# Rows turned in 32 by 32 squares: two of the kernel's transpose steps go from TensorE to transfers and VectorE

## The chip, the cores and the metric

The kernel runs on one core of a Trainium2 chip. The metric is the time of one execution on the device, in microseconds. The kernel before took 1190.43 us (median of three runs, 1189.83 to 1190.44). Its profile is that of one more execution, which took 1190.04 us.

The core has a matrix engine (TensorE, PE in the profile), a vector engine (VectorE, DVE), a scalar engine (ScalarE, ACT), a general one (GpSimd, POOL) and SyncE (SP), which here issues nearly all transfers. Each engine works through its own instructions in the order in which they were written; an instruction that waits holds up all that stand behind it on that engine. Transfers run on 16 DMA engines that all queues share.

## The reference

One layer of a hybrid decoder on 1024 tokens of width 1024, in float32:

```
h     = rmsnorm(x, mix_pre_norm)
proj  = h @ w_in                         # 1024 x 3584, split between two mixers
attn  = rmsnorm(dilated_mixture_attention(q_a, k_a, v_a), attn_out_norm)   # 512 wide
rec   = hgrn2_recurrence(q_h, f_h, i_h, g_h, ...)                          # 512 wide
mixed = concat([attn, rec]) @ w_out
x     = x + rmsnorm(mixed, mix_post_norm)
h     = rmsnorm(x, mlp_pre_norm)
ff    = square(relu(h @ w_ff1)) @ w_ff2   # inner width 4096
x     = x + rmsnorm(ff, mlp_post_norm)
```

Two places matter here. The product with `w_out` contracts over the 1024 columns of `[attn, rec]`, and the product with `w_ff1` over the 1024 columns of `h`. TensorE contracts over the partition axis, but both operands are made row by row, with tokens on partitions. So both have to be transposed first.

## The kernel before, in words

Every product is done in three passes: an operand is split into a high part (a rounded copy, by ScalarE) and a low part (the rest, by a VectorE subtraction). `split_into` (lines 85 to 87 before) does such a split; line 86 is the copy, line 87 the subtraction. `three_pass` (L90 to L92) is the three products.

Tokens are worked on in eight row blocks of 128, `t` = 0 to 7. The recurrence (`hgrn_core`, four heads) writes its gated rows to a buffer in device memory, `mix_dram` (L651), and the attention writes its own there too (`pair_rows`, L1134). The last quarter of the attention stays on the chip (`row_fin`).

The output stage is the loop over `t` from 0 to 7 after the attention (its steps are called step 0 to step 7 here). In step `t`, `late_out(t, 0)` and `late_out(t, 1)` multiply row block `t` with the two halves of `w_out`, 12 TensorE products each for the attention half, and 12 more each for the recurrent half where `t` is 4 or more. For `t` below 4 the recurrent half has been multiplied already during the attention (`early_out`, into `early_sum`). Between the two halves, `row_turn` makes the operands of the next row block: four TensorE transposes of 128 by 128 (L1208) into a PSUM bank, and a split of the bank.

Behind it, for each row, come a norm and the residual (`mixed_half`, `residual`, L1274 and L1275, on VectorE, with sums of squares on ScalarE and a power on POOL), the scaling for the feed-forward norm (`residual_b`, L1303, on VectorE), and `next_turn`: eight TensorE transposes (L1313) into two banks, and two ScalarE copies (L1319) into `hraw`, the transposed feed-forward operand. `split_tokens` splits it, 256 tokens at a time, into `h2`. Tables such as `RES`, `SCALE` and `TURN_END` say in which step each row has which of these done. Row 6 and row 7 are turned inside the first products of the feed-forward part (`mm1`).

After the loop, `mm1(0, 1)`, `mm1(1, 1)`, `mm1(0, 2)` and `mm1(1, 2)` are the first products with `w_ff1`, 12 instructions each, on tokens 0 to 511. The weight pairs that follow (`early_split(2)`, `early_split(3)`, written as wa2 and wa3) are split on ScalarE and VectorE; `early_mm(2, 1)` and `early_mm(3, 1)` use them. Tokens 512 to 1023 are split as `B22` after that.

A PSUM bank of `late_out` is used again by the row two steps later; for `t` of 4 or more it is free once `residual(t)` has read it. The order on all engines is the order in which the program is written out by hand; nothing moves instructions later. All loads and stores named here are issued by SP.

## Time and profile before

| | |
|---|---|
| median of three runs | 1190.43 us |
| profiled execution, its time | 1190.04 us |
| profiled execution, its span | 1188.1 us |
| TensorE busy | 1178.1 us (99%) |
| VectorE busy | 839.9 us (71%) |
| ScalarE busy | 548.9 us (46%) |
| POOL busy | 294.3 us (25%) |
| output stage and first feed-forward products | about 493 to 600 us of the span |

The span is the time from the first to the last instruction in the profile; the execution's own time has some 2 us beside it. In rows in order of time, the first number is the start in the span, the second a duration, both in us; `x8` is how many instructions were merged into the row, and what stands in brackets is idle time ahead of it and what ended it. Rows of groups give the duration as minimum, median and maximum in ns. Rows by stretch give, for PE, PEld, DVE, ACT and POOL in this order, the busy time and the number of instructions, and then the granted TensorE clock (1.00 is full speed), the share of the 16 DMA engines and GB/s.

### The profile page before, as it was taken

How to read it: one execution, taken by the hardware profiler on the slowest of the kernel's cores; microseconds unless marked ns; L12 is line 12 of the kernel's file. 1: busy time of each engine (PE TensorE's matmuls, PEld its weight loads, DVE VectorE, ACT ScalarE, POOL GpSimd, SP SyncE). 2: the span in 40 equal slices, each digit the busy share in tenths (PEclk: the TensorE clock that was granted, in tenths of full speed). 3: DMA queues.
4: the chain of work that ended last, by engine and by line, in shares of the span. 5: the costliest groups of instructions: out<-in, count | busy, mean ns of one | idle time of the engine just before them, and what ended most of it. 6: DMA issues, size and time to landing. Idle time of an engine off the chain costs nothing.

```text
span 1188.1 us, 17598 instructions
## 1 busy us (share of the span) xinstructions
PE 1178.1 (99%) x6486; PEld 1004.2 (85%) x6486; DVE 839.9 (71%) x1428; ACT 548.9 (46%) x1082; POOL 294.3 (25%) x282
## 2 busy tenths in 40 slices
PE   9999999999999999999999999999999999999997
PEld 9898989878888888888888888888888888888886
DVE  5686969686666667577697666675686653588796
ACT  7633424343666677764654222222244544434562
POOL 0112122001111010252503775667540000000022
PEclk9999999999999999999999999999999999999999
DMA  5222323147453644452425465554587524433337
GB/s 221 71 69 86 98 86 99 48 114 185 103 148 95 170 128 126 157 192 89 168 89 201 158 225 180 184 177 167 196 328 274 176 90 157 162 95 101 109 104 283
DMA packets 90549, 175.49 MB, mean 148 GB/s; under 512 B 14944, under 2 KB 42464, under 8 KB 90464
## 3 DMA queue, kind: packets, MB, share of 16 engines
q1 hardware_dynamic: 90320, 174.37, 45.4%
q8 instruction: 51, 0.84, 0.3%
q14 instruction: 34, 0.28, 0.1%
q10 hardware_dynamic: 144, 0.00, 0.0%
HBM read 116.91 MB, written 47.99 MB: 139 GB/s over the span
## 4 chain that ended last, share of the span: by engine, by line
PE 92%; ACT 3%; DVE 3%; issue 1%; DMA 0%; POOL 0%; DVEq 0%; POOLq 0%; ACTq 0%
PE f L2078 18%; PE f2s L2078 7%; PE pig L90 3%; PE pig L92 2%; PE pig L91 2%; PE pwo L90 2%; PE pwo L92 2%; PE pwo L91 2%; PE pl L536 1%; PE pm_ak L90 1%; PE pm_ak L92 1%; PE pm_ak L91 1%; PE pm_av L90 1%; PE pm_av L92 1%; PE pm_f L90 1%
## 5 line engine op out<-in xcount | busy, mean ns | idle before, releaser
L87 DVE TENSOR_TENSOR al<-ar,ah 128x1024 fp32r<-128x1024 f32 x56 | 70.7, 1262 | 79.7 <-ACT ah L86 77.4
L2078 PE MATMUL f<-bh,ah 128*128 128x512 f32 x320 | 124.5, 389 | 0.0
L2078 PE MATMUL f<-bl,ah 128*128 128x512 f32 x320 | 124.5, 389 | 0.0
L2078 PE MATMUL f<-bh,al 128*128 128x512 f32 x320 | 124.5, 389 | 0.0
L86 ACT ACTIVATE ah<-ar 128x1024 fp32r<-128x1024 f32 x56 | 59.1, 1056 | 86.8 <-DMA ar<-actd 86.4
L2078 PEld LDWEIGHTS f<-bh,ah 128*128 128x128 f32 x320 | 60.1, 188 | 12.6
L2078 PEld LDWEIGHTS f<-bl,ah 128*128 128x128 f32 x320 | 60.1, 188 | 12.5
L2078 PEld LDWEIGHTS f<-bh,al 128*128 128x128 f32 x320 | 60.1, 188 | 12.3
L2152 POOL TENSOR_SCALAR lbl<-ssq 128x1 f32<-128x1 f32 x4 | 3.3, 822 | 245.0 <-ACT fd L2148 244.8
L1701 POOL TENSOR_TENSOR e<-x,e 128x512 f32<-128x512 f32 x14 | 21.6, 1541 | 131.7 <-DVE x L1652 131.7
L2078 PE MATMUL f2s<-bh,al 128*128 128x512 f32 (+1 forms) x128 | 48.9, 382 | 0.0
L2078 PE MATMUL f2s<-bl,ah 128*128 128x512 f32 (+1 forms) x128 | 48.9, 382 | 0.0
L2078 PE MATMUL f2s<-bh,ah 128*128 128x512 f32 (+1 forms) x128 | 48.9, 382 | 0.0
L710 POOL TENSOR_SCALAR tout<-traw 128x256 f32<-128x256 f32 x16 | 19.2, 1199 | 103.0 <-DMA traw<-in_bias_tab_dram 100.2
L87 DVE TENSOR_TENSOR bl<-br,bh 128x1024 fp32r<-128x1024 f32 x32 | 40.1, 1255 | 1.1 <-ACT bh L86 1.0
L2095 ACT ACTIVATE acc<-f 128x512 f32<-128x512 f32 x28 | 16.7, 598 | 48.8 <-PE f L2078 48.8
L86 ACT ACTIVATE bh<-br 128x1024 fp32r<-128x1024 f32 x32 | 33.6, 1050 | 4.0 <-PE f L2078 3.0
L758 POOL TENSOR_TENSOR kl<-kf,kh 64x512 fp32r<-64x512 f32 x12 | 16.2, 1348 | 74.9 <-ACT kh L757 74.9
L90 PE MATMUL pwo<-woh,mt 128*128 128x512 f32 x80 | 32.2, 403 | 0.0
L87 DVE TENSOR_TENSOR wl<-raw,wh 128x1024 fp32r<-128x1024 f32 x21 | 25.7, 1224 | 8.6 <-ACT wh L86 8.6
L92 PE MATMUL pwo<-woh,mt 128*128 128x512 f32 x80 | 31.3, 391 | 0.0
L91 PE MATMUL pwo<-wol,mt 128*128 128x512 f32 x80 | 31.2, 390 | 0.0
(1725 smaller groups left out, 3882.7 us busy)
## 6 DMA issues: line engine op xcount, KB each, us to landing
ar<-actd SPq DMA_DIRECT2D x56, 512.0 KB, 3.6
br<-in_w_ff_dram SPq DMA_DIRECT2D x16, 1024.0 KB, 5.8
raw<-in_w_in_dram SPq DMA_DIRECT2D x28, 512.0 KB, 3.9
w1r<-in_w_ff_dram SPq DMA_DIRECT2D x14, 1024.0 KB, 6.4
actd<-e SPq DMA_DIRECT2D x17, 768.0 KB, 4.2
actd<-e SPq DMA_DIRECT2D x11, 1024.0 KB, 4.1
xr<-in_x_dram SPq DMA_DIRECT2D x8, 512.0 KB, 8.1
raw<-in_w_out_dram SPq DMA_DIRECT2D x8, 512.0 KB, 3.9
```

The lines of the kernel that those rows point to most:

```text
L86: S.activation(hi, src, AF.Copy)
L87: eng.tensor_tensor(out=lo, in0=src, in1=f32(hi), op=ALU.subtract)
L90: TE.matmul(dst, lhs[0], rhs[0], start=start, stop=False)
L91: TE.matmul(dst, lhs[0], rhs[1], start=False, stop=False)
L92: TE.matmul(dst, lhs[1], rhs[0], start=False, stop=stop)
L536: TE.matmul(pl[a:b, n, :96], kt[:, (4 * u + n) * P + a:(4 * u + n) * P + b], qs[:, :, 32 * g:32 * g + 32], start=True, stop=True, skip_gro ...
L710: G.tensor_scalar(by_class(dst[:, part_ * w:(part_ + 1) * w]), in_blocks(raw[:, FAR * DIL:]), 8.0, None, op0=ALU.mult)
L758: G.tensor_tensor(out=kl[a:b], in0=src, in1=f32(kh[a:b]), op=ALU.subtract)
L1701: eng[0].tensor_tensor(out=e1[:, 3], in0=a21, in1=e1[:, 2], op=ALU.add)
L2078: TE.matmul(pm, a[:, j, c], b[:, j, d], start=start and j == 0 and q == 0, stop=stop and j == 1 and q == 2, skip_group_check=True)
L2095: S.activation(acc_at(p, i), pm, AF.Copy)
L2152: G.tensor_scalar(base[:, t:t + 1], sums[j][:, t:t + 1], 1.0 / D, EPS, op0=ALU.mult, op1=ALU.add)
```

## The change

A transpose of 128 by 128 can be done in two steps: move its sixteen squares of 32 by 32 to their transposed places, and turn each square in itself. The change does the first step with transfers and the second with an instruction of VectorE that turns every 32 by 32 square of a tile (`V.transpose`, listed as STREAM_TRANSPOSE).

For the recurrent half of the mixer rows, the recurrence now writes to a buffer of its own (`rec_dram`), and `squares_load` reads it back in squares, in four transfers, one for each group of 32 partitions; a contiguous run is 32 floats, 128 B. This takes the place of a plain load. `row_turn` for that half becomes one turn on VectorE and a split that reads from SBUF. There is one `squares_load` for each two of rows 0 to 3 and one each for rows 4 to 7.

For the feed-forward rows 0 to 6, `residual_b` is followed by a store of the scaled row to device memory (`x2n_dram`). `lay_out` reads it back in squares, again in four transfers of 128 B runs, into the place where it was, and `square_turn` turns it on VectorE, in two instructions, right into `hraw`. Row 7 is still transposed by `next_turn`. `square_turn` stands later than `next_turn` did: rows 0, 1, 2 and 4 in the middle of the next step, row 3 at the end of step 6, row 5 after `mm1(0, 1)`, row 6 after `mm1(0, 2)`. The first `split_tokens` goes from step 5 to step 6.

```diff
@@ -254,8 +254,10 @@
 
     pick4 = cp.tile([P, DIL], F32, name="pick4")
     pick32 = cp.tile([P, 32], F32, name="pick32")
-    mix_dram = dp.tile([T, D], F32, name="mixd")
+    mix_dram = dp.tile([T, AW], F32, name="mixd")
+    rec_dram = dp.tile([T, AW], F32, name="recd")
     x2_dram = [dp.tile([P, D], F32, name=f"x2d{t}") for t in range(NT)]
+    x2n_dram = [dp.tile([P, D], F32, name=f"x2nd{t}") for t in range(NT - 1)]
 
     def ig_evac(hd, pm, blocks):
         for u, t in enumerate(blocks):
@@ -648,7 +650,7 @@
                 V.scalar_tensor_tensor(gate[:, n], pos[n // 4][:, n % 4], rs[:, n:n + 1], gate[:, n],
                                        op0=ALU.mult, op1=ALU.mult)
             if g2 == 3:
-                nc.sync.dma_start(out=mix_dram[:, h * P:(h + 1) * P].rearrange("(n p) d -> p n d", p=P), in_=gate)
+                nc.sync.dma_start(out=rec_dram[:, h * P:(h + 1) * P].rearrange("(n p) d -> p n d", p=P), in_=gate)
         if h == HH - 1:
             look(0, "N", 0)
             return gated
@@ -1129,7 +1131,7 @@
                         in1=recips[pr][:, :, b].rearrange("p h j -> p j h").unsqueeze(3).to_broadcast([P, 4, 2, 64]),
                         op=ALU.mult)
         if hf == 1:
-            to = mix_dram[:, AW + pr * P:AW + (pr + 1) * P].rearrange("(n i r) d -> r i n d", r=DIL, i=32)
+            to = mix_dram[:, pr * P:(pr + 1) * P].rearrange("(n i r) d -> r i n d", r=DIL, i=32)
             for r in range(DIL):
                 nc.sync.dma_start(out=to[r], in_=anats[pr][32 * r:32 * r + 32].rearrange("p n i d -> p n (i d)"))
 
@@ -1147,14 +1149,19 @@
     def early_rows():
 
 
-        early["rows"] = wide.tile([P, NE, AW], F32, tag="A", name="erows")
+        early["rows"] = wide.tile([P, NE // 2, 4, 2 * P], F32, tag="A", name="erows")
         early["table"] = wide.tile([P, 2, T], F32, tag="A", name="etable")
         early["order"] = early["table"][:, 1, :P]
         G.tensor_copy(early["order"].rearrange("p (i r) -> p i r", r=DIL), ident.rearrange("p (r i) -> p i r", r=DIL))
         early["mt"] = [wide.tile([P, 2, 2, 4, P], F32R, tag="A", name=f"emt{q}") for q in range(NE // 2)]
         for q in range(NE // 2):
-            nc.sync.dma_start(out=early["rows"][:, 2 * q:2 * q + 2],
-                              in_=mix_dram[2 * q * P:2 * (q + 1) * P, :AW].rearrange("(n p) d -> p n d", p=P))
+            squares_load(early["rows"][:, q], 2 * q, 2)
+
+    def squares_load(dst, t0, n):
+
+        src = rec_dram[t0 * P:(t0 + n) * P].rearrange("(b r) (j g f) -> g r j b f", r=32, g=4, f=32)
+        for g in range(4):
+            nc.sync.dma_start(out=dst[32 * g:32 * g + 32].rearrange("p j (b f) -> p j b f", f=32), in_=src[g])
 
     def early_sums():
         early["sum"] = [wide.tile([P, 2, D], F32, tag="A", name=f"esum{q}") for q in range(NE // 2)]
@@ -1164,11 +1171,14 @@
 
     def row_load(t):
         row = rows[t] = slab("S", f"row{t}")
-        c = AW if t < NE else 0
-        nc.sync.dma_start(out=row[:, c:AW + AL], in_=mix_dram[t * P:(t + 1) * P, c:AW + AL])
+        if t >= NE:
+            squares_load(rec_row(t), t, 1)
+        nc.sync.dma_start(out=row[:, AW:AW + AL], in_=mix_dram[t * P:(t + 1) * P, :AL])
 
     def rec_row(t):
-        return early["rows"][:, t] if t < NE else rows[t][:, :AW]
+        if t < NE:
+            return early["rows"][:, t // 2, :, t % 2 * P:(t % 2 + 1) * P]
+        return rows[t][:, :AW].rearrange("p (j c) -> p j c", j=4)
 
     def row_fin(t):
         return anats[-1][:, t].rearrange("p i d -> p (i d)")
@@ -1201,10 +1211,14 @@
                 mts[t] = slab("V8", f"mt{t}", F32R, (P, 2, 2, 4, P))
             dst = mts[t][:, which]
         mts[t, which] = dst
-        src = rec_row(t) if which == 0 else rows[t][:, AW:]
+        if which == 0:
+            V.transpose(rec_row(t), rec_row(t))
+            split_into(dst[:, 0], dst[:, 1], rec_row(t))
+            return
+        src = rows[t][:, AW:]
         pt = bank("pv" if late else tag, f"pmt{t}_{which}")
         for j in range(4):
-            piece = row_fin(t) if which == 1 and j == 3 else src[:, j * P:(j + 1) * P]
+            piece = row_fin(t) if j == 3 else src[:, j * P:(j + 1) * P]
             TE.transpose(pt[:, j * P:(j + 1) * P], piece, ident)
         split_into(dst[:, 0], dst[:, 1], pt.rearrange("p (j c) -> p j c", j=4))
 
@@ -1302,6 +1316,30 @@
             xress[t] = slab("S", f"x2n{t}")
         V.scalar_tensor_tensor(xress[t], xr, scales.pop(("x2", t)), gains["gmlp"], op0=ALU.mult, op1=ALU.mult)
 
+    def raw_room(t):
+        th = t // 4
+        if t % 4 == 0:
+            for kh in range(2):
+                hraw[kh, th] = wide.tile([P, 4, 512], F32, tag="A", name=f"hraw{kh}{th}")
+                if th == 0:
+                    h2[kh] = tuple(wide.tile([P, 4, 512], F32R, tag="A", name=f"h2{q}{kh}") for q in "hl")
+
+    def lay_out(t):
+
+        src = x2n_dram[t].rearrange("(a r) (k g f) -> g r k a f", a=4, g=4, f=32)
+        for g in range(4):
+            nc.sync.dma_start(out=xress[t][32 * g:32 * g + 32].rearrange("p (k a f) -> p k a f", k=NK, a=4), in_=src[g])
+
+    def square_turn(t):
+
+        xr = xress.pop(t)
+        th, c = t // 4, (t % 4) * P
+        raw_room(t)
+        for kh in range(2):
+            V.transpose(hraw[kh, th][:, :, c:c + P], xr[:, kh * 512:kh * 512 + 512].rearrange("p (k c) -> p k c", k=4))
+        if t == 4:
+            x_again(7)
+
     def next_turn(t):
 
         xr = xress.pop(t)
@@ -1312,10 +1350,6 @@
                 k = kh * 4 + j
                 TE.transpose(pt[:, j * P:(j + 1) * P], xr[:, k * P:(k + 1) * P], ident)
             src = pt.rearrange("p (j c) -> p j c", j=4)
-            if t % 4 == 0:
-                hraw[kh, th] = wide.tile([P, 4, 512], F32, tag="A", name=f"hraw{kh}{th}")
-                if th == 0:
-                    h2[kh] = tuple(wide.tile([P, 4, 512], F32R, tag="A", name=f"h2{q}{kh}") for q in "hl")
             S.activation(hraw[kh, th][:, :, c:c + P], src, AF.Copy)
 
     def split_tokens(kh, c):
@@ -1451,11 +1485,14 @@
     SCALE = {3: (0,), 4: (1,), 5: (2,), 6: (4,), 7: (5,)}
     SCALE_MID = {7: (6,)}
     SCALE_END = {5: (3,)}
-    TURN_MID = {6: (3,)}
-    TURN_END = {3: (0,), 4: (1,), 5: (2,), 6: (4,), 7: (5,)}
+    LAY_MID = {6: (3,)}
+    LAY_END = {3: (0,), 4: (1,), 5: (2,), 6: (4,), 7: (5,)}
+    TURN_MID = {4: (0,), 5: (1,), 6: (2,), 7: (4,)}
+    TURN_END = {6: (3,)}
 
     def scaled(r):
         residual_b(r)
+        nc.sync.dma_start(out=x2n_dram[r], in_=xress[r])
         if r + 3 < NT and r != 4:
             x_again(r + 3)
 
@@ -1480,23 +1517,23 @@
             x_again(t + 1)
         if NE <= t + 2 < NT:
             row_attn(t + 2)
-        if t in (5, 7):
+        if t in (6, 7):
             for kh in range(2):
-                split_tokens(kh, (t - 5) * P)
+                split_tokens(kh, (t - 6) * 2 * P)
         for r in RES.get(t, ()):
             residual(r)
+        for r in LAY_MID.get(t, ()):
+            lay_out(r)
+        mixed_half(t, 0)
         for r in TURN_MID.get(t, ()):
-            next_turn(r)
-        mixed_half(t, 0)
+            square_turn(r)
         late_out(t, 1)
         for r in SCALE_MID.get(t, ()):
             scaled(r)
         if t == NT - 1:
             w_get(W10 + 1, 0)
-        for r in TURN_END.get(t, ()):
-            next_turn(r)
-            if r == 4:
-                x_again(7)
+        for r in LAY_END.get(t, ()):
+            lay_out(r)
         if t + 3 < NT:
             row_norm(t + 3)
         if t == 4:
@@ -1506,6 +1543,8 @@
             residual(r)
         for r in SCALE_END.get(t, ()):
             scaled(r)
+        for r in TURN_END.get(t, ()):
+            square_turn(r)
 
 
 
@@ -1790,7 +1829,9 @@
     mm1(0, 1, "a", True)
     out_p1(0)
     residual(NT - 1)
-    mm1(1, 1, "a", True, lambda: next_turn(NT - 2), 1)
+    lay_out(NT - 2)
+    square_turn(NT - 3)
+    mm1(1, 1, "a", True)
     out_p1(1)
     small.add("S")
     residual_b(NT - 1)
@@ -1800,6 +1841,7 @@
     early_load(4)
     mm1(0, 2, "a", False)
     out_p2(0)
+    square_turn(NT - 2)
     for tag in ("T", "BT"):
         small.add(tag)
     mm1(1, 2, "a", False, lambda: next_turn(NT - 1), 2)
```

TensorE loses 88 instructions and its order is otherwise as before. On SP, the stretch that follows the loads of the last rows is, before, from row 3's `x2d` store on:

```order
L1293 DMA x2d_137<-xres_6034 128x1024
L1248 DMA xres_6288<-in_x_dram 128x1024
L1293 DMA x2d_138<-xres_6152 128x1024
L1248 DMA xres_6378<-in_x_dram 128x1024
L1293 DMA x2d_139<-xres_6288 128x1024
L1248 DMA xres_6493<-in_x_dram 128x1024
L1293 DMA x2d_140<-xres_6378 128x1024
```

Now, from row 3's scaled store on (`x2nd_146` to `x2nd_149` are the scaled rows 3 to 6, `x2d_140` and `x2d_141` the residuals of rows 5 and 6; `x4` is the four transfers of a row's squares):

```order
L1495 DMA x2nd_146<-esum_5161 128x1024
L1262 DMA xres_6360<-in_x_dram 128x1024
L1495 DMA x2nd_147<-xres_6150 128x1024
L1307 DMA x2d_140<-xres_6283 128x1024
L1331 DMA esum_5161<-x2nd_146 32x32x32 x4
L1331 DMA xres_6150<-x2nd_147 32x32x32 x4
L1495 DMA x2nd_148<-x2n_6495 128x1024
L1307 DMA x2d_141<-xres_6360 128x1024
L1262 DMA xres_6527<-in_x_dram 128x1024
L1495 DMA x2nd_149<-x2n_6554 128x1024
L1331 DMA x2n_6495<-x2nd_148 32x32x32 x4
```

Row 3's square loads stand behind the store of row 5's residual, and row 5's behind the store of row 6's scaled row. On VectorE, from the end of row 5's residual in step 6 on, there stood before:

```order
L1275 TENSOR_TENSOR xres_6288<-ad_6427,xres_6288 128x512
L1303 SCALAR_TENSOR_TENSOR x2n_6528<-xres_6288,x2r_6433,gmlp 128x1024
L87 TENSOR_TENSOR h2l_6091<-hraw_6089,h2h_6090 128x4x256
L87 TENSOR_TENSOR h2l_6100<-hraw_6098,h2h_6099 128x4x256
L1274 SCALAR_TENSOR_TENSOR ad_6534<-pwo_0_6380,prp_6498,gpost 128x512
```

Now the turns of rows 2 and 3 stand between (both in `esum_5161`):

```order
L1289 TENSOR_TENSOR xres_6283<-ad_6410,xres_6283 128x512
L1339 STREAM_TRANSPOSE hraw_6196<-esum_5161 128x4x128
L1339 STREAM_TRANSPOSE hraw_6199<-esum_5161 128x4x128
L1339 STREAM_TRANSPOSE hraw_6196<-esum_5161 128x4x128
L1339 STREAM_TRANSPOSE hraw_6199<-esum_5161 128x4x128
L1317 SCALAR_TENSOR_TENSOR x2n_6495<-xres_6283,x2r_6416,gmlp 128x1024
L87 TENSOR_TENSOR h2l_6198<-hraw_6196,h2h_6197 128x4x256
L87 TENSOR_TENSOR h2l_6201<-hraw_6199,h2h_6200 128x4x256
L1288 SCALAR_TENSOR_TENSOR ad_6502<-pwo_0_6362,prp_6463,gpost 128x512
```

Row 5's scaling, the splits and row 6's residual now stand behind row 3's turn. After the loop, from the end of row 7's residual on, VectorE had before:

```order
L1275 TENSOR_TENSOR xres_6493<-ad_6650,xres_6493 128x512
L1303 SCALAR_TENSOR_TENSOR x2n_6688<-xres_6493,x2r_6656,gmlp 128x1024
L87 TENSOR_TENSOR wa2l<-wr_6618,wa2h 128x1024
L87 TENSOR_TENSOR wa3l<-wr_6620,wa3h 128x1024
L87 TENSOR_TENSOR B220l<-hraw_6491,B220h 128x1024
```

Now it has, with the turn of row 5 (`x2n_6495`) and that of row 6 (`x2n_6554`):

```order
L1289 TENSOR_TENSOR xres_6527<-ad_6617,xres_6527 128x512
L1339 STREAM_TRANSPOSE hraw_6523<-x2n_6495 128x4x128
L1339 STREAM_TRANSPOSE hraw_6524<-x2n_6495 128x4x128
L1317 SCALAR_TENSOR_TENSOR x2n_6649<-xres_6527,x2r_6623,gmlp 128x1024
L87 TENSOR_TENSOR wa2l<-wr_6585,wa2h 128x1024
L1339 STREAM_TRANSPOSE hraw_6523<-x2n_6554 128x4x128
L1339 STREAM_TRANSPOSE hraw_6524<-x2n_6554 128x4x128
L87 TENSOR_TENSOR wa3l<-wr_6587,wa3h 128x1024
L87 TENSOR_TENSOR B220l<-hraw_6524,B220h 128x1024
```

Row 7's scaling (`x2n_6649`) stands behind row 5's turn, and the split of the weight pair wa3 behind row 6's.

## The prediction

> **What bounds the kernel now.** I read the page's busy times and chain first, then the busy times by stretch around the changed stage, then TensorE's and VectorE's rows in order of time, and last the transfers.
>
> ```profile
> span 1188.1 us, 17598 instructions
> PE 1178.1 (99%) x6486; PEld 1004.2 (85%) x6486; DVE 839.9 (71%) x1428; ACT 548.9 (46%) x1082; POOL 294.3 (25%) x282
> PE 92%; ACT 3%; DVE 3%; issue 1%; DMA 0%; POOL 0%; DVEq 0%; POOLq 0%; ACTq 0%
> 450.00:470.00 20.00, 19.44 (x135) 16.94 (x134) 14.82 (x43) 15.27 (x45) 0.80 (x2) 1.00 0.65 174
> 500.00:510.00 10.00, 10.00 (x50) 8.27 (x49) 5.55 (x8) 4.59 (x17) 4.44 (x11) 1.00 0.93 353
> 540.00:550.00 10.00, 10.00 (x50) 8.34 (x49) 8.02 (x10) 4.59 (x12) 2.34 (x5) 1.00 0.32 107
> 570.00:580.00 10.00, 10.00 (x51) 8.33 (x50) 5.47 (x7) 6.55 (x15) 4.11 (x8) 1.00 0.82 308
> ```
>
> TensorE is the bound: 92% of the chain, and from 500 us on it has no idle time in a stretch. So each microsecond taken out of its queue there is a microsecond of the kernel, and so is each microsecond for which it is made to wait: nothing behind the stage has slack in which a wait could vanish. VectorE is busy 55 to 80% of these stretches, and the DMA engines (the column before the last, as a share of 16) have room except around 500 to 510 us.
>
> **What is removed.** One step of eight transposes, and all transposes that go:
>
> ```profile
> 518.10 0.40 PE L92 MATMUL pwo<-woh,mt 128*128 128x512 f32 x1
> 518.33 1.04 PE L1313 MATMUL ph<-ident,esum 128*128 128x128 f32 x8
> 519.12 0.47 PE L90 MATMUL pwo<-woh,mt 128*128 128x512 f32 x1
> 519.44 0.39 PE L91 MATMUL pwo<-wol,mt 128*128 128x512 f32 x1
> L1313 PE MATMUL ph<-ident,esum x32: 272/272/273, 518.3 to 551.7; 128*128 128x128 f32 x32
> L1208 PE MATMUL pmt<-ident,erows x16: 272/273/329, 441.6 to 466.4; 128*128 128x128 f32 x16
> ```
>
> The listed 272 ns overlap, so cadence counts. A product follows the one before by 0.227 us (518.10 to 518.33); from 518.33 to 519.44 lie eight transposes and one product, 1.11 us, so eight transposes cost 0.885 us and four 0.44. Seven of eight feed-forward rows go (7 x 0.885 = 6.2) and the recurrent halves of rows 4 to 7 (4 x 0.44 = 1.76): **7.95 us** in the stage without idle time. The 16 for rows 0 to 3, another 1.8, lie at 441 to 466 us, where TensorE is 97% busy and VectorE gets 4 turns more (2.4 us by the price below). I bound this by -1.8 and +2.4 and take -0.5, nearer to TensorE's own row. The build shows 88 transposes fewer on TensorE, so that the change does not do what it says is no rival.
>
> **What a turn on VectorE costs.** The trace has no 32 by 32 turn. Nearest are operations from SBUF to SBUF:
>
> ```profile
> 510.68 0.41 DVE L1192 TENSOR_SCALAR row<-row,ara 128x384 f32<-128x384 f32 x1
> 515.64 1.28 DVE L1303 SCALAR_TENSOR_TENSOR esum<-xres,x2r,gmlp 128x1024 f32<-128x1024 f32 x1
> 553.34 0.69 DVE L1275 TENSOR_TENSOR xres<-ad,xres 128x512 f32<-128x512 f32 x1
> ```
>
> 384 elements a partition take 0.41 us and 512 take 0.69 (0.61 from start to start). I take 0.6 for 512, between 0.41 and 1.28. There are 8 for the mixer and 14 for the feed-forward rows, beside work on an engine with 20 to 45% free; where it is not free, it is in the walk below.
>
> **What a row in squares costs.** A feed-forward row is stored whole, and read back by four transfers of 1024 packets of 128 B: 4096 packets, 256 on each DMA engine. Rows for the price:
>
> ```profile
> x2d<-xres SPq DMA_DIRECT2D x8, 512.0 KB, 3.7
> traw<-in_bias_tab_dram SPq DMA_DIRECT2D x64, 32.0 KB, 2.1
> DMA packets 1139, 0.12 MB, mean 159 GB/s; under 512 B 1069, under 2 KB 1129, under 8 KB 1138
> DMA packets 1039, 0.52 MB, mean 268 GB/s; under 512 B 15, under 2 KB 1039, under 8 KB 1039
> ```
>
> The third row is the 0.75 us from 70.90 us, filled with packets of 4 B: 0.75 x 16 / 1139 = 10.5 ns each. The fourth is the 1.96 us from 120.90 us, 1024 packets of 512 B: 30 ns each. Between them by bytes, 128 B cost 15 ns, and 256 of them 3.9 us (2.7 to 7.7). A load of two packets an engine lands after 2.1 us, nearly all fixed. So the four land 2.0 + 3.9 = **5.9 us** after the first is issued (4.7 to 9.7), and none is issued before the store has landed, 3.7 us.
>
> The Trainium skill (DMA: Bandwidth & Descriptors, Specifications) says that below 512 B a transfer leaves line rate, by a read-modify-write. The trace has 17 GB/s an engine at 512 B, and 128 B at the price of 512 B would be my upper end, 9.7 us, and a sum near 1217.
>
> **Where the time goes: five waits of TensorE.** SP issues in order and VectorE works in order. A turn that waits for its row holds all VectorE work behind it, and a row's loads stand on SP behind stores that wait for VectorE. I walk through the order with the trace's durations: 0.13 for a hand-over, and for one half of an output row 12 products, 2.72 us (24 from row 4 on). The same walk without the change gives no wait.
>
> ```profile
> 550.73 1.09 ACT L86 ACTIVATE mt<-pmt 128x512 fp32r<-128x512 f32 x2 [2.14 <-PE pmt L1208]
> 552.57 0.74 DVE L1274 SCALAR_TENSOR_TENSOR ad<-pwo,prp,gpost 128x512 f32<-128x512 f32 x1
> 557.00 0.55 POOL L83 TENSOR_TENSOR x2r<-ms,nhalf 128x1 f32<-128x1 f32 x1
> 558.10 0.47 PE L90 MATMUL pwo<-woh,mt 128*128 128x512 f32 x1
> 560.59 2.36 DVE L87 TENSOR_TENSOR h2l<-hraw,h2h 128x1024 fp32r<-128x1024 f32 x2 [1.72 <-ACT h2h L86]
> 567.88 1.29 DVE L1303 SCALAR_TENSOR_TENSOR x2n<-xres,x2r,gmlp 128x1024 f32<-128x1024 f32 x1 [2.03 <-POOL x2r L83]
> 577.72 2.31 DVE L1303 SCALAR_TENSOR_TENSOR x2n<-xres,x2r,gmlp 128x1024 f32<-128x1024 f32 x1 [2.04 <-POOL x2r L83]
> 580.45 1.03 PE L1313 MATMUL ph<-ident,x2n 128*128 128x128 f32 x8
> 583.15 0.39 PE L1635 MATMUL f12a<-h2h,wa2l 128*128 128x512 f32 x1
> L86 ACT ACTIVATE h2h<-hraw x4: 1062/1066/1073, 539.0 to 560.4; 128x1024 fp32r<-128x1024 f32 x4
> ```
>
> One, step 4. Row 4's recurrent half is turned after the scaling that ends at 516.9, then copied by ScalarE (0.6) and subtracted (0.6): with hand-overs ready at 519.0. TensorE, without two batches of transposes, asks at 517.9: 1.1 us.
>
> Two, step 7. It begins at 558.10 now; 6.2 less of transposes and 1.1 of waiting make it 552.9. Its bank is freed by the first operation of row 5's residual (552.57 now), and the split of the first 256 tokens, 2.5 us, has moved from step 5 to right ahead of it. VectorE ends row 7's operands at 551.2 and the split at 553.7, the bank is free at 554.5: 1.6 us.
>
> Three, the first feed-forward product. Row 5's residual ends at 556.5, and only then can SP pass its store and issue row 3's loads: from 557.4 they land at 563.8 (5.9, and half a microsecond for row 4's beside them). VectorE holds row 3's turn since 557.7, nothing passes it, and turn, row 5's scaling (1.2) and the split end at 567.5. TensorE asks at 565.4: 2.1 us.
>
> Four, row 7's transposes (580.45 now). From 568.6 VectorE has row 6's residual (2.9), row 4's turn (1.2), 1.0 until POOL has row 6's scale, and its scaling, to 574.9. Row 6's store follows, and row 5's loads stand behind it on SP: issued at 575.7, landed at 582.2. Their turn is ahead of row 7's scaling, so row 7 is ready at 584.8. TensorE has done its three and a half products by 577.1: 7.7 us.
>
> Five, the second weight pair's product. Row 6's loads are issued after the store of row 7's residual, at 582.6, behind six weight loads of 512 KB. By the stretch 570 to 580 (308 GB/s at a share of 0.82) each takes 1.4 us of all engines, so the squares land at 595.0. Row 6's turn stands ahead of the pair's split on VectorE: ready at 597.5. TensorE comes there at 589.8: 7.8 us.
>
> Sum: 1.1 + 1.6 + 2.1 + 7.7 + 7.8 = 20.3 of waiting, less 7.95 and 0.5, is +11.9. The profiled execution took 1190.04 us, 0.39 below the median 1190.43 and inside the runs shown: 1190.0 + 11.9 = **1202 us**. Waits three to five each grow with the landing time one for one: at 4.7 us the sum is 1198, at 9.7 it is 1213, and 1217 with what then waits for banks as well. A turn of 0.4 instead of 0.6 takes 1.6 off; one of 1.28 adds some 5. The mixer's loads (2048 small packets each, around 500 us, where the share is already 0.93) delay the gains loaded behind them by 1 to 2 us; VectorE stands idle there for 3.0 us, which covers them:
>
> ```profile
> 504.14 0.69 DVE L87 TENSOR_TENSOR mt<-pmt,mt 128x512 fp32r<-128x512 f32 x1 [3.04 <-ACT mt L86]
> ```
>
> **Rivals.** *The loads are hidden*, 15%: no turn is ever waited for, and only 7.95 and 0.5 remain: 1181.6 us. For it: VectorE's free 20 to 45%, and half a step between most loads and turns. It holds only if rows 3, 5 and 6 land before VectorE reaches them; even at 4.7 us the walk has row 5's turn waiting 2 us and row 6's 8, which is why it has so little.
>
> *Half of it is covered*, 8%: if the last two turns stall VectorE but TensorE is made to wait only half as long as I say (10 instead of 20), loss and gain nearly cancel: 1190.0 + 10.2 - 8.45 = 1192 us.
>
> *The waits slow TensorE itself*, 15%: after each of the two long waits the next 12 products run at half speed, 5.4 instead of 2.7 us: 1202 + 5.4 = 1207 us. Against it: no row shows a slower clock, the clock column is 1.00 in all stretches; but no stretch has such a wait either. The Trainium skill (TensorE: Matmul & The Clock Gate, Part 1: The HAM clock gate) has this rule: after an idle window of about 3.4 us the clock halves, until some 3.4 us of work have passed. No run here shows it; by its own figure I estimate 1.7 us a wait, 1205 us.
>
> **Chances.** The five waits as walked 62%, halved clock 15%, hidden loads 15%, cancelled 8%. The five waits alone give 1197 to 1217; the range goes down to 1187 to take in the cancelled case, and leaves out the hidden one and a small part above. A difference under 0.2% (2.4 us) is not told from none by a measurement of this kernel; by the same cases faster has 17%, same 6%, slower 77%.
>
> **What would show it.** Right: TensorE idle between 550 and 610 us, with two gaps of several microseconds, at row 7's transposes and at the product with the second weight pair, ended by VectorE, and VectorE's own idle time there ended by the square loads. Landing of the four loads of a row near 6 us from the first issue; a 512-wide turn near 0.6 us; TensorE's busy time some 10 us smaller. Wrong: a gapless TensorE in that stretch (then the loads land early, or VectorE has more lead than I give it), turns above 1 us, or idle time around 425 to 510 us from the small packets, to which I gave nothing.

## The result, and the profile after

The changed kernel took 1206.66 us (median of four runs, 1206.17 to 1207.56), the kernel before 1190.41 beside it: a ratio of 1.0139 (95% interval 1.0126 to 1.0151), 1.4% slower. The forecast was 1202, with 1187 to 1217 as its range. The direction, the cause and the place of the wait that decides were as forecast. The 4.7 us that were missing are, to 0.1 us, TensorE's clock (2.9 us), which was a rival with 15%, and the end of that wait, 1.9 us later than the walk has it.

The profiled execution took 1206.17 us. Its page, with the engines' busy times and the chain of waits:

```profile
span 1204.4 us, 17517 instructions
...
PE 1176.6 (98%) x6398; PEld 998.2 (83%) x6398; DVE 848.5 (70%) x1450; ACT 542.3 (45%) x1068; POOL 289.1 (24%) x282
...
PE 49%; DVE 2%; SPq 1%; DMA 1%; issue 1%; ACT 0%; POOL 0%; DVEq 0%; POOLq 0%; ACTq 0%
```

TensorE has less work (88 instructions fewer), and the span is 16.3 us longer. The waits of TensorE between 540 and 610 us (who waits, for what; in sum, how often, the longest):

```profile
PE f13a L1674 <- DVE wa3l L87: 8.7, 1, 8.7
PE f11a L1672 <- ACT wh L86: 3.6, 1, 3.6
PE f11a L1674 <- DVE wl L87: 1.4, 1, 1.4
PE pwo L90 <- DVE ad L1288: 1.1, 1, 1.1
PE f10a L1673 <- DVE h2l L87: 0.5, 1, 0.5
```

And its busy time by stretch, with the granted clock in the third column from the right:

```profile
570.00:580.00 10.00, 5.03 (x14) 3.41 (x13) 8.21 (x11) 4.75 (x12) 2.91 (x6) 0.74 0.74 200
580.00:590.00 10.00, 10.00 (x47) 8.27 (x46) 3.70 (x4) 6.65 (x11) 2.90 (x5) 0.92 0.99 336
590.00:600.00 10.00, 1.34 (x5) 0.84 (x4) 3.76 (x4) 2.60 (x3) 8.09 (x7) 0.76 0.59 149
600.00:610.00 10.00, 10.00 (x34) 8.00 (x33) 5.97 (x6) 3.73 (x5) 0.00 (x0) 0.73 0.03 11
```

The gapless stage has two holes, at the second first-layer product (f11a, two waits one after the other) and at the third weight pair's (f13a, which waits for wa3l), and the clock column falls with each. The rows of TensorE in order of time show the price. Behind the second hole, products follow each other at 0.43 us instead of 0.23:

```profile
599.46 0.80 PE L1674 MATMUL f13a<-h2h,wa3l 128*128 128x512 f32 x1 [8.66 <-DVE wa3l L87]
600.05 0.63 PE L1672 MATMUL f13a<-h2h,wa3h 128*128 128x512 f32 x1
600.48 0.63 PE L1673 MATMUL f13a<-h2l,wa3h 128*128 128x512 f32 x1
...
605.55 0.39 PE L1673 MATMUL f12a<-h2l,wa2h 128*128 128x512 f32 x1
```

From 599.46 to 605.55 lie 14 products, 6.09 us; at 0.227 they take 3.18: 2.9 us lost. Behind the first hole's second wait 12 products from 576.27 to 581.56 take 5.29 instead of 2.72: 2.6 lost.

What sets the end of the long wait is not TensorE at all. The chain that ended last, in order of time (start, length, what; pieces of a few hundredths to 0.54 us between these are left out):

```profile
583.12 0.57 SPq L1331
...
583.74 4.77 SPq L1331
...
588.55 3.85 SPq L1331
...
592.45 3.67 DMA x2n<-x2nd
...
596.87 0.67 DVE hraw L1339
597.54 1.87 DVE wa3l L87
```

Row 6's four square loads (L1331) hold SP for 10 us behind the weight loads; the last lands at 596.1, VectorE turns the row, and only then splits the weights that TensorE has waited for since 590.8. VectorE's own rows show it, and the same for row 3:

```profile
564.12 1.30 DVE L1339 STREAM_TRANSPOSE hraw<-esum 128x512 f32<-128x512 f32 x2 [4.89 <-DMA esum<-x2nd]
...
596.24 1.30 DVE L1339 STREAM_TRANSPOSE hraw<-x2n 128x512 f32<-128x512 f32 x2 [10.28 <-DMA x2n<-x2nd]
```

### The profile page after: what moved, and what is told of

It is laid out like the page before. It is cut to its first block, busy times and chain, and to the rows that moved or that the text cites. A ratio compares the mean times of both kernels' runs of the same rounds, so it can differ in the third digit from the quotient of the medians.

```text
span 1204.4 us, 17517 instructions
## 1 busy us (share of the span) xinstructions
PE 1176.6 (98%) x6398; PEld 998.2 (83%) x6398; DVE 848.5 (70%) x1450; ACT 542.3 (45%) x1068; POOL 289.1 (24%) x282
## 4 chain that ended last, share of the span: by engine, by line
PE 49%; DVE 2%; SPq 1%; DMA 1%; issue 1%; ACT 0%; POOL 0%; DVEq 0%; POOLq 0%; ACTq 0%
PE f L2120 18%; PE f2s L2120 7%; SPq L1331 1%; DMA x2n<-x2nd 1%; DVE ad L1288 0%; DVE xres L1289 0%; DVE h2l L87 0%; DMA x2d<-xres 0%; DMA esum<-x2nd 0%; PE f13a L1674 0%; DVE x2n L1317 0%; DVE hraw L1339 0%; PE f13a L1673 0%; PE f13a L1672 0%; DVE wa3l L87 0%
## 5 line engine op out<-in xcount | busy, mean ns | idle before, releaser
L2120 PEld LDWEIGHTS f<-bh,ah 128*128 128x128 f32 x320 | 60.1, 188 | 12.4
L2120 PEld LDWEIGHTS f<-bl,ah 128*128 128x128 f32 x320 | 60.1, 188 | 12.4
```

The lines of the kernel that those rows point to most:

```text
L2120: TE.matmul(pm, a[:, j, c], b[:, j, d], start=start and j == 0 and q == 0, stop=stop and j == 1 and q == 2, skip_group_check=True)
```

## The experiments

Twelve kernels, each beside the kernel before on the same chip. The medians of before were 1190.39 (first four runs), 1190.20 (next four) and 1190.24 us (last four). None leaves a part of the computation out.

**1. Is the slow clock the idle time's work?** Extra products, thrown away, fill both holes:

```diff
+        for _ in range(fill):
+            TE.matmul(pm, ops1[q - 1][1][0][:, :P], part_of(b, 0)[0], start=True, stop=True, ...)
...
-    mm1(1, 1, "a", True)
+    mm1(1, 1, "a", True, fill=25)
...
-            mm1(q, 1, "a", True)
+            mm1(q, 1, "a", True, fill=48 if q == 3 else 0)
```

> The changed kernel, with extra products that are thrown away where TensorE stands still: 25 (5.7 us) ahead of the product that waits for the second weight pair's split at 570 us, and 48 (10.9 us) ahead of the one that waits from 590.6 to 599.5. Nothing else is changed and nothing is left out. Theory A, idle time slows TensorE's clock: the products behind both waits now follow each other at 0.227 us instead of 0.427, the clock column is 1.00 in all stretches, and the time falls by 2.9 us only, to 1203.8: the 2.6 us that the first wait's clock cost are eaten by the second wait, whose end VectorE sets. Theory B, the slow products have another cause (the transfers that run beside them): they stay slow, and the time stays at 1206.7.

Measured: 1205.73 us. The clock was full in all stretches, but only 0.9 us came back: the fill ended at 601.6, 1.3 us behind the split, and VectorE waited 1.7 us for a gain vector (until 510.5 us), for which it does not wait in the changed kernel's trace. So it was run again with 40 instead of 48.

> As the run with thrown-away products in the two gaps, but 40 instead of 48 in the second, so that they end at 599.8 us, just before the split that TensorE waits for there (600.3), and not 1.3 us behind it (601.6) as measured. Theory A, the clock behind the last wait costs 2.9 us: full clock everywhere, a wait of under 1 us at that product, and 1203.8 us (1203 to 1205). Theory B, the clock's loss is covered by something later: 1205.7 or more again, at a full clock.

Measured: 1204.45 us (1203.46 to 1205.62), 2.2 us under the changed kernel. The stretch of the first hole:

```profile
570.00:580.00 10.00, 10.00 (x46) 8.26 (x45) 8.33 (x11) 4.04 (x10) 2.90 (x6) 1.00 0.61 189
```

And TensorE's rows behind the second fill:

```profile
600.58 0.39 PE L1674 MATMUL f13a<-h2h,wa3h 128*128 128x512 f32 x1
600.81 0.39 PE L1675 MATMUL f13a<-h2l,wa3h 128*128 128x512 f32 x1
```

0.23 us a product, and the same transfers beside it: the idle time slows the clock, theory B falls. That 5.5 us of lost clock are worth 2.2 and not 5.5 is the second reading: what TensorE gains behind the first hole it loses in the second, whose end VectorE sets. That the last 2.9 did not come back whole has a reason in the same trace: the split was ready at 600.9, 1.5 us later than in the changed kernel.

**2. Is the 8.7 us wait a place in SP's queue?** Row 6's loads ahead of the four raw weights:

```diff
     early_load(3)
+    lay_out(NT - 2)
     for q in range(2):
         q_raw[q] = [small.get(f"w1r{q}{f}") for f in range(2)]
...
-    lay_out(NT - 2)
     square_turn(NT - 3)
```

> The changed kernel, with row 6's four square loads issued ahead of the four 512 KB loads of the raw first weights (and of row 7's residual store), right behind the two weight loads that are split next. Theory A, the 8.7 us wait is a place in SP's queue: the squares land near 587 instead of 596 us, the wait for the third weight pair's split falls below 1 us, no clock is lost behind it, and the time is 1195 (1193 to 1198). Theory B, small packets are what is slow, wherever they stand: they land at 593 or later, the wait shrinks by 3 us at most, and the time is 1203 or more.

Measured: 1200.10 us (ratio 1.0080, 1.0063 to 1.0097). SP's rows for row 6's loads and for the raw weights behind them:

```profile
580.44 5.16 SPq L1331 DMA_DIRECT2D x2n<-x2nd  x4
585.64 2.75 SPq L1829 DMA_DIRECT2D w1r<-in_w_ff_dram  x4
```

VectorE's row for its turn:

```profile
589.85 1.30 DVE L1339 STREAM_TRANSPOSE hraw<-x2n 128x512 f32<-128x512 f32 x2 [3.52 <-DMA x2n<-x2nd]
```

And TensorE's waits between 540 and 640 us, those under 1 us left out:

```profile
PE f11a L1672 <- ACT wh L86: 3.6, 1, 3.6
PE f13a L1674 <- DVE wa3l L87: 1.4, 1, 1.4
PE pwo L90 <- DVE ad L1288: 1.3, 1, 1.3
PE f10c L1672 <- ACT wf01h L86: 1.0, 1, 1.0
```

The wait fell from 8.7 to 1.4 and took its slow clock with it, so its cause is the place, as theory A says; the time lies between the two theories. For the row landed at 589.7, not 587, the raw weights that had to make room came some 4 us later (POOL begins their sums at 592.3 instead of 588.0), and these sums now hold TensorE up at f10c. A transfer that is moved ahead pushes another one back: 6.6 us were won, not the 11.7 expected.

**3. Which rows have no lead?** (A row has a lead when its squares land before VectorE reaches its turn.) Rows 3, 5 and 6 back on TensorE, at their places of before:

```diff
-    LAY_MID = {6: (3,)}
-    LAY_END = {3: (0,), 4: (1,), 5: (2,), 6: (4,), 7: (5,)}
+    LAY_MID = {}
+    LAY_END = {3: (0,), 4: (1,), 5: (2,), 6: (4,)}
...
-    TURN_END = {6: (3,)}
+    TURN_END = {}
...
+        if t == 6:
+            next_turn(3)
...
+        if t == 7:
+            next_turn(5)
...
+    mm1(1, 1, "a", True, lambda: next_turn(NT - 2), 1)
```

> The changed kernel, with rows 3, 5 and 6 turned on TensorE at their places of before; rows 0, 1, 2 and 4 and the recurrent half stay in squares. Theory A, only these three rows have no lead: the waits of 3.6, 1.4, 8.7 and 0.5 us and both stretches of slow clock are gone, one of 1.1 us may stay. Against before: +1.7 for rows 0 to 3 of the mixer (measured up to 466 us), -1.8 for rows 4 to 7, -3.5 for four rows, +1.4 of small waits, so 1188 us (1187 to 1190). Theory B, VectorE's added work as such holds TensorE: waits of several us between 550 and 590 remain, and the time is above 1192.

Measured: 1188.63 us (ratio 0.9984, 0.9975 to 0.9993). Two waits are left between 540 and 640 us, 0.6 and 0.2 us, at a full clock. These three rows are the whole loss, 18 us; the four with a lead pay.

**4. What do rows 0 to 3 of the mixer cost?** The same, with their recurrent half loaded plainly and transposed on TensorE.

> As the run before it (rows 3, 5 and 6 on TensorE), and the recurrent half of rows 0 to 3 on TensorE as well, with plain loads. What is left in squares: the recurrent half of rows 4 to 7 and feed-forward rows 0, 1, 2 and 4. Theory A, the turn of rows 0 to 3 costs VectorE more than it saves TensorE: 1.7 us less than the run before it, 1186.5 (1185 to 1188), TensorE's shift at 466 us is 0. Theory B, the 1.7 us came from the 4096 small packets on the DMA queues around 422 to 440 us or chance: still gone, since those are gone too; but if rows 0 to 3 gain what their 16 transposes take (1.8 us), it is 1.8 us slower, 1190.

Measured: 1186.94 us (ratio 0.9971, 0.9960 to 0.9982), 1.7 us less than run 3, as theory A says; TensorE's rows are shifted against those of before by 1.5 us more at 475 us than at 440 us in run 3, and by 0.1 here. To see why, the changed kernel's group of operations on that tile, how long ScalarE then waited for the turn (erows), and VectorE for ScalarE's copy (emt):

```profile
L1215 DVE STREAM_TRANSPOSE erows<-erows x4: 699/702/712, 442.9 to 468.4; 128x512 f32<-128x512 f32 x4
L86 ACT ACTIVATE emt<-erows x4: 629/630/634, 443.6 to 469.2; 128x512 fp32r<-128x512 f32 x4
...
  DVE erows L1215: 3.5, 4
  ACT emt L86: 2.8, 4
```

VectorE turns for 0.70 us and then stands still for 0.70 (2.8 in four) until ScalarE's copy is done, because the other half of that split is next in its order. So each turn and the wait behind it take 1.4 us. Not all of that is the change's: before, where TensorE transposes, VectorE already stands still at the same splits, by its waits from 440 to 475 us:

```profile
DVE emt L87 <- ACT emt L86: 2.2, 3, 0.9
```

The change adds 2.8 us of turns and 0.6 of standing still, on an engine that is busy 82% from 442 to 470 us (22.94 of 28.00 us; not the 97% of the expectation below). The test is to turn one step of the attention loop earlier, on the kernel of run 3:

```diff
-        45: lambda: wo_half(1, 1),
+        45: lambda: [wo_half(1, 1), rec_turn(0)],
...
-        49: lambda: [load_bias(AH - 1), wo_half(3, 0)],
+        49: lambda: [load_bias(AH - 1), wo_half(3, 0), rec_turn(1)],
+        51: lambda: rec_turn(2),
+        53: lambda: rec_turn(3),
```

> As the run with feed-forward rows 3, 5 and 6 on TensorE and all mixer rows in squares (1188.6 us measured), but VectorE turns the recurrent half of rows 0 to 3 one step of the attention loop ahead of the split that uses it. Theory A: in the changed kernel VectorE turns for 0.7 us and then stands still for 0.7 us, since next on it is the second half of the split, which waits for ScalarE's copy; with the turn ahead, the 0.7 us of standing still go, TensorE's shift at 466 us falls from 1.7 to 0.9 or less, and the time to 1187.8. Theory B, only the turn's own time on a VectorE that is 97% busy there counts, or the loads: 1188.6, as measured.

Measured: 1187.40 us, 1.2 us less. The same group there:

```profile
L1209 DVE STREAM_TRANSPOSE erows<-erows x4: 701/704/712, 442.1 to 466.1; 128x512 f32<-128x512 f32 x4
...
  ACT emt L86: 0.7, 2
```

The turn costs what it did; the standing still fell from 2.8 to 0.7 us, and TensorE's shift from 440 to 475 us from 1.5 to 0.1. The small packets are all still loaded in this run, so they were not the cause: most of the 1.7 us was the order, not the turn. But the 16 transposes taken off TensorE there, 1.8 us by the prediction's price, pay nothing even so.

**5. The recurrent half alone.** The kernel before with only `squares_load` and the turns of the eight mixer rows:

> The kernel before with the recurrent half of all eight mixer rows in squares and nothing of the feed-forward rows: all of these on TensorE as before. Theory A, this half of the change cancels in itself: +1.7 us for rows 0 to 3, -1.8 for rows 4 to 7, +0.3 for one wait: 1190.6 (1190 to 1191.5), no idle time of TensorE above 1 us after 490. Theory B, the 8192 small packets around 500 to 520 us delay the gains and rows too: waits there, and 1192 or more.

Measured: 1191.88 us (ratio 1.0014, 1.0005 to 1.0024), 1.3 above the forecast of theory A and just below that of theory B. Two waits of TensorE, 0.7 us at 546 (VectorE's residual is late) and 0.6 at 559 (ScalarE's copy of a transposed row is late), ate what rows 4 to 7 saved. VectorE does wait 1.0 us for a gain at 509 us, but it stands idle for 4.1 us more before that late residual, so theory B is near in time without its reason.

**6. Three tries to keep more rows in squares.** Row 5 late (run 4's kernel with row 5's turn behind the third pair's split); all squares with only the order mended; and rows 0 to 5 in squares with row 3's loads ahead of row 5's residual and row 5's turn late. The order in the second one:

```diff
+        for r in LAY_MID.get(t, ()):
+            lay_out(r)
         for r in RES.get(t, ()):
             residual(r)
-        for r in LAY_MID.get(t, ()):
-            lay_out(r)
...
     early_split(3)
+    square_turn(NT - 3)
+    square_turn(NT - 2)
     out_p2(1)
```

> As the run with rows 3, 5 and 6 and the mixer's rows 0 to 3 on TensorE (1186.9 us measured), but row 5 is in squares again, with its turn on VectorE moved behind the split of the third weight pair, where nothing of the first products waits for it. Theory A, a late row is harmless when no other work stands behind its turn: one batch of transposes less, 0.9 us, so 1186.1 (1185.5 to 1187). Theory B, its four loads, ahead of the weight loads on SP, delay these: a wait of 1 to 3 us for the second or third pair's split, and 1187.5 or more.

> The changed kernel with all its squares, three places changed: row 3's loads are issued ahead of row 5's residual instead of behind it, row 6's ahead of the four raw first weights (as in the run that gave 1200.1), and the turns of rows 5 and 6 stand behind the split of the third weight pair. Theory A, the loss lies in the order on SP and VectorE alone: the waits of 3.6, 1.4 and 8.7 us and the slow clock are gone; what stays is 1.7 us for rows 0 to 3 of the mixer and some 2 us where the raw weights come later; less 8.0 for all transposes: 1187 (1185 to 1190). Theory B, small packets and VectorE's added turns have no room in this stage: waits of more than 5 us in sum remain, and it is above 1192.

> Rows 0 to 5 of the feed-forward part in squares, row 3's loads ahead of row 5's residual, row 5's turn behind the split of the third weight pair; row 6, and the recurrent half of rows 0 to 3, on TensorE. Theory A: against the run with rows 3, 5 and 6 on TensorE (1186.9) two batches less, 1.8 us: 1185.2 (1184.5 to 1186.5), with no wait of TensorE above 1 us between 550 and 600. Theory B, row 3 is late even so: VectorE waits at its turn, the first product waits for the split behind it, and the time is 1187 or more.

Measured: 1188.68 us (ratio 0.9989, 0.9979 to 0.9998), 1197.27 (1.0055, 1.0040 to 1.0070) and 1189.64 (0.9995, 0.9985 to 1.0004). All three missed theory A, by 2.6, 10 and 4.4 us. The order alone gives back 9.4 us of the 16 (1206.66 to 1197.27), and then the waits sit elsewhere. The longest waits of TensorE in the second kernel:

```profile
PE f14a L1672 <- ACT wa4h L86: 1.7, 1, 1.7
PE f11a L1674 <- DVE wl L87: 1.4, 1, 1.4
PE f11a L1672 <- ACT wh L86: 1.2, 1, 1.2
PE f10c L1672 <- ACT wf01h L86: 1.0, 1, 1.0
```

And what ScalarE waited for there:

```profile
ACT wa4h L86 <- DMA wr<-in_w_ff_dram: 3.8, 1, 3.8
ACT wf01h L86 <- POOL s L1862: 3.8, 1, 3.8
```

Weight loads that stand behind the squares come late (wa4, and wf01 by way of POOL's sums): theory B's figure was the nearer one there. In the last kernel row 3 was still 1.6 us late for VectorE; but TensorE's longest wait in the first and the last is not at the squares' next user, as theory B had it. TensorE waits for the weight split of f11a: 1.2 and 1.4 us for its second half (wl), and in the last kernel 1.1 more for its first (wh). VectorE's and ScalarE's work of that step decides, and a transpose taken off TensorE there makes it wait longer: in run 4, with row 5 on TensorE, the same wait is 0.3 us, 0.9 less than in the first.

**7. The best of it.** Run 4's kernel with the turns of rows 4 to 7 ahead of the feed-forward scaling, so that ScalarE copies while VectorE scales; and, beside it, feed-forward rows 0, 1, 2 and 4 alone:

```diff
+        if NE <= t + 1 < NT:
+            rec_turn(t + 1)
         for r in SCALE.get(t, ()):
             scaled(r)
```

> As the run with rows 3, 5 and 6 and the mixer's rows 0 to 3 on TensorE (1186.9 us measured), but the recurrent half of rows 4 to 7 is turned ahead of the feed-forward scaling of that step instead of behind it, so that ScalarE's copy runs beside the scaling. Theory A, the 0.75 us for which VectorE waits for this copy in each step come back as earlier splits: the waits of 0.2 to 0.3 us at 520, 571 and 577 go, 1186.3 (1185.8 to 1187). Theory B, these waits have another cause: 1186.9.

> Feed-forward rows 0, 1, 2 and 4 in squares, everything else on TensorE: the recurrent half is loaded plainly and transposed on TensorE for all rows. Theory A, the recurrent half of rows 4 to 7 pays beside the feed-forward rows what TensorE's order shows, 0.44 us a row: 1188.4, 1.5 us slower than with it (1186.9). Theory B, it pays nothing, as the run with the recurrent half alone suggests (1191.9, of which rows 0 to 3 explain 1.7): 1186.9.

Measured: 1185.89 us (1184.63 to 1186.26; ratio 0.9961, 0.9948 to 0.9973) and 1186.42 (1185.88 to 1186.60; 0.9968, 0.9955 to 0.9980). The first beats the kernel before by 0.4%, and the changed one by 20.8 us. The wait at 520 us is gone, but those of f11a stay, and TensorE's waits from 500 to 610 us are 0.8 us in sum, where run 4's trace has 0.7. So theory A's time came without its reason, and where the microsecond between the two runs lies is not shown:

```profile
PE f11a L1687 <- DVE wl L87: 0.6, 1, 0.6
PE f11a L1685 <- ACT x L1707: 0.2, 1, 0.2
```

The second has no wait of TensorE there at all. So the recurrent half of rows 4 to 7 pays nothing beside the four rows as the change places it (1186.9 with it, 1186.4 without), and some 0.5 us with the turns ahead, which the intervals do not separate from nothing.

## Why the prediction was right, and where it was off

**The transposes saved** were sized right. In the kernel with four feed-forward rows alone, the first product behind each of them shifts by 0.8 to 0.9 us more (0.885 forecast). TensorE's busy time fell by 1.5 us all the same and not by some 10: the products at half clock take back 5.5, and the rest was not followed up.

**Rows 0 to 3 of the mixer** failed, in sign: -0.5 was taken, between -1.8 and +2.4, and TensorE's shift at 475 us was +1.7, of which 0.2 stand already at 300 us, where nothing is changed. The step that failed is the choice near TensorE's own row, as if transposes taken off it must pay there: run 10 (the turn ahead) gets 1.4 of the 1.5 us back by the order alone, and the transposes pay nothing with either order. The price of a turn as 0.6 us left out the wait for ScalarE behind it.

**A turn of 0.6 us** measured 0.69 to 0.70, 0.61 from start to start where two follow each other. Right.

**The landing**: 5.9 us after the first issue was forecast, and row 3's turn began 5.7 us after it (558.45 to 564.12), row 5's 5.8. But the two parts of that number were both wrong and made up for each other, which is luck. In the 0.80 us from 562.50 us, filled with nothing but packets of 128 B, there were 1341 of them:

```profile
DMA packets 1341, 0.17 MB, mean 212 GB/s; under 512 B 1341, under 2 KB 1341, under 8 KB 1341
```

And SP's rows for four square loads and for the store of a whole row:

```profile
558.45 3.14 SPq L1331 DMA_DIRECT2D esum<-x2nd  x4
...
571.79 0.33 SPq L1307 DMA_DIRECT2D x2d<-xres  x1
```

So a packet costs 9.5 ns an engine (0.80 x 16 / 1341), not 15; and a row's four issues alone take SP 3.1 us, 0.8 each, where a whole row's store takes 0.33. I had no term for that. The Trainium skill (DMA: Bandwidth & Descriptors, Specifications) expects transfers below 512 B to fall off line rate by a read-modify-write. Here 128 B moved at 13.4 GB/s an engine, beside 17 at 512 B before: a quarter less, where the upper end of the landing time (9.7 us) stood for the same 30 ns a packet as at 512 B. That end was far off.

**The five waits** were forecast as 1.1, 1.6, 2.1, 7.7 and 7.8, 20.3 in sum; measured are 0.3, 1.1, 0.5, 5.0 and 8.7, 15.6. The fourth was in another place: not at row 7's transposes but at f11a. Its weights (wh) are copied by ScalarE, and the copy stands there behind the sums of squares of row 6's residual (L1302), which stood behind row 3's turn on VectorE:

```profile
571.85 0.63 ACT L1302 ACTIVATE dx<-xres 128x512 f32<-128x512 f32 x1 [0.71 <-DVE xres L1289]
...
573.05 1.04 ACT L86 ACTIVATE wh<-raw 128x1024 fp32r<-128x1024 f32 x1
```

The walk had left ScalarE's queue out. With the first hole filled, the wait appears at row 7's transposes too (1.65 us). The fifth was right in place and cause: squares landed at 596.1 (595.0 forecast), the split was ready at 599.4 (597.5 forecast). Since this wait's end decides, the errors in the others did no harm. The 1.9 us by which it was late are 1.1 of landing (the loads were issued 0.5 us later, and took 13.0 us from the first issue instead of 12.4) and 0.8 of turn and split (the split took 1.9 us; in run 2 it took 1.2). How much of it comes from rows 0 to 3 is not shown: row 5's residual ended 1.5 us late (558.0, 556.5 forecast), but at the end of row 6's scaling 0.2 us of that were left (575.1, 574.9 forecast), and no run has the changed kernel with those rows alone on TensorE.

**The gains** behind the mixer's loads were covered, as forecast, in the changed kernel's trace; in those of the first fill run and of the recurrent half alone VectorE waited 1.7 and 1.0 us for one.

**The clock**: the forecast took it as full, with the slow clock as a rival at 15%, 1207 us. It happened. By the walk, the last wait ends 11.7 us later than the same product starts before (585.87), which is nearly the sum's 11.9. So 1202 + 1.9 (the end of that wait) + 2.9 (the clock behind the last wait) is 1206.8, and 1206.66 was measured. The argument against it, that no row of before shows a slower clock, was empty, as the prediction itself said: before has no wait of that length. The rival's working (12 products at half speed behind each of two waits) was right behind each hole, but charged the first one as well, which costs nothing; it came out at 1207 because the 1.9 us of the late split were missing in it, and that is luck.

**The hidden loads** (1181.6) and the half-covered case (1192) did not occur, though run 3 shows what the first would need: rows with a full step between load and turn are hidden, as the four of that run are.

## What to carry to other kernels

Work taken off the busiest engine pays only where its replacement has a lead; sort the pieces by their lead and move those alone: four of seven rows gave 3.5 to 4.4 us, all of them cost 16. An in-order engine pays for what stands next to the new instruction as much as for the instruction itself: put it where the engine would not have to wait for its successor's other input. And several waits along one engine do not add up: find the one whose end another chain sets, and charge what lies behind it.

## What the runs showed of the hardware

- TensorE's clock halves behind idle time; the fill runs show that it is the idle time. In the changed kernel it was at one half from 574.8 to 581.6 us and from 595.2 to 605.5 us (rows by stretch just inside these, the clock third from the right):

```profile
574.80:581.50 6.70, 5.31 (x13) 4.15 (x13) 4.49 (x7) 2.37 (x6) 2.37 (x6) 0.50 0.95 229
...
595.30:605.40 10.10, 5.94 (x14) 4.70 (x15) 5.43 (x5) 3.27 (x4) 3.02 (x3) 0.50 0.15 53
```

  These stretches are 6.8 and 10.2 us long; a third one, in the kernel with rows 0 to 5 in squares, is 3.4 us long (from 573.3 us). That is two, three and one times some 3.4 us. The fall does not come at once: the two products between the waits of 3.6 and 1.4 us (574.15 and 574.48) took 0.50 and 0.40 us, as after a short wait at full clock, and in the long hole the clock fell 4.4 us after TensorE stopped at 590.8. Waits of 3.6 and 1.4 us, of 3.6 and 0.9 (run 2) and of 8.7 us did it; one of 2.4 us (in the second fill run, at 557 us) did not. A pair of waits of 1.1 and 1.4 us, 0.7 us apart, did it in one kernel and not in another, by the rows of both:

```profile
572.32 0.50 PE L1676 MATMUL f11a<-h2h,wl 128*128 128x512 f32 x1 [1.38 <-DVE wl L87]
...
575.04 0.63 PE L1674 MATMUL f11a<-h2h,wh 128*128 128x512 f32 x1
```

```profile
572.43 0.51 PE L1674 MATMUL f11a<-h2h,wl 128*128 128x512 f32 x1 [1.38 <-DVE wl L87]
...
573.47 0.40 PE L1672 MATMUL f11a<-h2h,wh 128*128 128x512 f32 x1
```

  The first is the kernel with rows 0 to 5 in squares, the second the one with all squares and the order mended. The other three executions of the second took 1.5 to 2.3 us more at a mean clock of 0.996 beside 0.998, as if it had come there too; they have no trace. The Trainium skill (TensorE: Matmul & The Clock Gate, Part 1: The HAM clock gate) says that the clock is set by a window of some 3.4 us that runs freely. The lengths of the stretches agree with that, and so does a pair of waits that halves the clock once and once not. The Trainium skill names at least one idle window as the condition. That differs here: in the kernel with rows 0 to 5 in squares TensorE stood still for only 1.7 us of the 3.4 us before the fall (busy for 1.62 of the 3.30 us from 569.90). The half clock lasted for 5.3 and 6.1 us of work in the changed kernel, so the loss was 2.6 and 2.9 us and not the 1.7 that the prediction estimated from one such window.
- Packets of 128 B cost 9.5 ns each, about the 10.5 of packets of 4 B before: at this size the number of packets is the price, not the bytes.
- A transfer's issue can hold SP for microseconds: one of row 6's took 4.8 us behind 3 MB of weight loads, where those of rows 3 to 5 took 0.6 to 0.9 and those of rows 0 to 2 up to 2.1. Why it is held was not tried apart.
